# Latent attention rewritten with keys on the partitions: row maxima from a separate product, the shift as two contraction rows, no turning of the probabilities

## The chip, the cores and the metric

The kernel runs on one core of a Trainium2 chip. The metric is the device time of one execution in microseconds (us), the median of several runs. The engines are called PE (matrix product; PEld is its weight load), DVE (vector), ACT (activation), POOL (GpSimd) and SP (the queue that issues most DMAs). Each engine works through its instructions in the order in which the program was written out for it.

## The reference

The reference is a two-layer decoder trunk. Layer 0 mixes tokens with a windowed attention, layer 1 with a multi-head latent attention, and each mixer is followed by a mixture of experts. Only the latent attention is touched. It computes, for 16 heads over 2048 tokens, with queries and keys of 64 + 32 features and values of 64:

```
q = concat(q_nope, rope(q_rope)); k = concat(k_nope, rope(k_rope, shared by all heads))
sc = einsum('bqhd,bkhd->bhqk', q, k) * 96 ** -0.5
sc = where(kpos <= qpos, sc, -inf)
p = softmax(sc, axis=-1)
o = einsum('bhqk,bkhd->bqhd', p, v);  out = o.reshape(b, s, 1024) @ w_o
```

## The kernel before

All products are made from float16 pairs: a number is kept as a high part and a low part, and a product is three matmuls (high by high, high by low, low by high). The latent attention has two parts. `latents` makes the compressed latents, the queries (left in DRAM as `q`) and the shared rotary keys (`kr`). `attend`, which the change rewrites, loops over heads.

In `attend` a unit is one head `h` and one tile `i` of 128 queries; queries lie on the partitions. `scores` makes the scores of a unit in chunks of up to 512 keys: three matmuls into a PSUM bank (`sc`, a ring of 7 that `room` hands out), a fourth on the diagonal that adds the causal mask, and a maximum over the chunk on DVE (L1401). When the last chunk is there, a second small maximum joins them (L1406), and only then ACT takes the exponential with the negated maximum as its bias (L1410, `bpr`). The second product needs keys on the partitions, so the probabilities are turned. Four fifths of them are split first, high part by DVE or ACT (L1425, L1427), low part by POOL or DVE (L1428), packed (`bpp`) and turned by a DMA from SBUF to SBUF (`send`, L186, `bpt`). One fifth (`direct`) is turned by PE (`turn_unit`, L1440), and then split from PSUM by ACT and DVE (L1444, L1445, `bpd`). `values` runs LAG = 6 units behind: for each block of 128 keys one matmul of the high part with 130 columns and one of the low part with 65 (L1459, L1460) into `po`, which DVE sums over its two halves (L1466).

Keys and values of the next pair of heads are projected in between (`pair`, its matmuls are L202 to L204, its splits L177 and L182), in the rooms of the same ring. `finish` divides by the sums, turns and stores a pair of heads to `ob`; `deliver` loads a head's queries into `qb` from DRAM. The list `todo` spreads these pieces over the units.

The program text gives instructions their priority. A planner then writes out each engine's order beforehand, and may bring forward an instruction that it takes to be ready. On the chip every engine keeps that order.

Of the kernel before, what the change touches and what calls it, by code (L numbers as in the profile page):

```python
# [20 lines left out]
S, D = 2048, 1024  # L21
# [105 lines left out]
class Kernel:  # L127
# [994 lines left out]
    def mla(self, x1_d, y_d, x2_d, d, keep):  # L1122
# [17 lines left out]
        with self.tc.tile_pool(name="hw", bufs=2, side="right", reuse_waits="tile") as self.hw:  # L1140
            self.latents(x1_d, y_d, x2_d, d["kr"], d["q"])
            self.attend(d["q"], d["kr"], d["ob"], rooms)
# [186 lines left out]
    def attend(self, q_d, kr_d, o_d, w_o):  # L1329
        nc, tc = self.nc, self.tc  # L1330
        V, G, C = nc.vector, nc.gpsimd, nc.scalar
        LAG, PACK, SHARES, TURNED = 6, 8, (2 / 5, 1 / 16), 1 / 5
        with ExitStack() as s:
# [4 lines left out]
            kb = [self.t(kp, [96, 2, S], F16, f"kb{n}") for n in range(3)]  # L1338
            qb = [self.t(kp, [96, 2, S], F16, f"qb{n}") for n in range(2)]
            for n in range(3):  # L1340
                nc.sync.dma_start(kb[n][NOPE:], kr_d)
            U, heads, todo, owed = {}, {}, [], [0.0, -150.0, 0.0]

            pack = {"n": 0}

            def room():
                return self.t(ps, [P, 512], F32, "sc", bufs=7)

            def place(nb):
                if pack["n"] + nb > PACK:  # L1350
                    send()
                if pack["n"] == 0:
                    pack["pp"] = self.t(wk, [P, PACK, 2, P], F16, "bpp", bufs=8)
                    pack["pt"] = self.t(wk, [P, PACK, 2, P], F16, "bpt", bufs=9)
                at = pack["n"]
                pack["n"] += nb
                return pack["pp"][:, at:at + nb], pack["pt"][:, at:at + nb]

            def send():
                n, pp, pt = pack["n"], pack["pp"], pack["pt"]  # L1360
                if n:
                    self.turn(pt[:, :n].rearrange("p k s q -> p (k s) q"), pp[:, :n].rearrange("p k s q -> p (k s q)"))
                pack["n"] = 0
# [9 lines left out]
            def direct(h, i, w):  # L1373

                owed[2] += TURNED * w
                if h == B_H - 1 and i >= 13:
                    return True
                if owed[2] > w / 2:
                    owed[2] -= w
                    return True  # L1380
                return False

            def scores(n, h, i, u, c):

                (Qh, Ql), (Kh, Kl) = ([b[h % len(b)][:, x] for x in range(2)] for b in (qb, kb))
                qs = slice(i * P, (i + 1) * P)
                nk = (i + 1) * P
                ncn = -(-nk // 512)
                if c == 0:
                    u["sm"], u["sc"], u["pt"], u["pr"] = self.t(wk, [P, 8], F32, "bsm2", bufs=4), [], [], []  # L1390
                sm = u["sm"]
                w = min(512, nk - 512 * c)
                ks = slice(512 * c, 512 * c + w)
                sc = room()
                last = c == ncn - 1
                nc.tensor.matmul(sc[:, :w], Qh[:, qs], Kh[:, ks], start=True, stop=False)  # L1396
                nc.tensor.matmul(sc[:, :w], Qh[:, qs], Kl[:, ks], start=False, stop=False)  # L1397
                nc.tensor.matmul(sc[:, :w], Ql[:, qs], Kh[:, ks], start=False, stop=not last)  # L1398
                if last:
                    nc.tensor.matmul(sc[:, w - P:w], self.ident_b, self.causal, start=False, stop=True)  # L1400
                V.tensor_reduce(sm[:, c:c + 1], sc[:, :w], axis=AX.X, op=ALU.max, negate=ncn == 1)  # L1401
                u["sc"].append((sc, w))
                if not last:
                    return
                if ncn > 1:
                    V.tensor_reduce(sm[:, 4:5], sm[:, 0:ncn], axis=AX.X, op=ALU.max, negate=True)  # L1406
                nm = sm[:, 4:5] if ncn > 1 else sm[:, 0:1]
                for sc, w in u["sc"]:
                    pr = self.t(wk, [P, 512], F32, "bpr", bufs=7)
                    C.activation(pr[:, :w], sc[:, :w], AF.Exp, bias=nm)  # L1410
                    if direct(h, i, w):
                        u["pr"].append((len(u["pt"]), pr, w))
                        u["pt"].append(None)
                        continue
                    pp, pt = place(w // P)
                    u["pt"].append(pt)
                    pb = pr[:, :w].rearrange("p (k q) -> p k q", q=P)

                    mine = [False, False]
                    for part, share in enumerate(SHARES):  # L1420
                        owed[part] += share * w
                        if owed[part] > w / 2 and not (part and mine[0]):
                            mine[part], owed[part] = True, owed[part] - w
                    if mine[0]:
                        V.tensor_copy(pp[:, :, 0], pb)  # L1425
                    else:
                        C.activation(pp[:, :, 0], pb, AF.Copy)  # L1427
                    (V if mine[1] else G).tensor_tensor(pp[:, :, 1], pb, pp[:, :, 0], op=ALU.subtract)  # L1428
                if n % 2 and (h == B_H - 1 or n == len(units) - 1):
                    send()  # L1430

            def turn_unit(u):

                many = len(u["pr"]) > 1
                for c, pr, w in u["pr"]:
                    if many and c % 2 == 0:
                        two = self.t(wk, [P, PACK, 2, P], F16, "bpt", bufs=9)
                    tp = room()
                    for k in range(0, w, P):
                        nc.tensor.transpose(tp[:, k:k + P], pr[:, k:k + P], self.ident)  # L1440
                    out = two[:, c % 2 * 4:] if many else self.t(wk, [P, 4, 2, P], F16, "bpd", bufs=5)
                    out = u["pt"][c] = out[:, :w // P]
                    tp = tp[:, :w].rearrange("p (k q) -> p k q", q=P)
                    C.activation(out[:, :, 0], tp, AF.Copy)  # L1444
                    V.tensor_tensor(out[:, :, 1], tp, out[:, :, 0], op=ALU.subtract)  # L1445

            def values(h, i, n, u, c):

                second = n % 2
                j = units[n ^ 1][1]  # L1450
                if c == 0 and not second:
                    U["po"] = self.t(ps, [P, 512], F32, "po", bufs=1)
                slot = i > j
                po = U["po"][:, slot * 130:(slot + 1) * 130]
                v = self.vbs[h // 2 % 2]
                pt = u["pt"][c]
# [52 lines left out]
            for n in range(len(units) + LAG):  # L1509
# [24 lines left out]
                for c in range(max(ns, nv)):  # L1534
                    if c < ns:
                        scores(n, h, i, U[n], c)
# [121 lines left out]
```

## Time and profile before

| | |
|---|---|
| median of 3 runs | 3584.36 us (3579.23 to 3592.11) |
| the profiled execution | 3587.38 us, of which the span of the profile is 3585.3 us |
| mean granted PE clock | 0.928 of full speed |
| busy in the span | PE 2972.7, DVE 2785.0, ACT 2105.8, POOL 1564.5 us |
| latent attention (`attend`) | about 1684 to 2550 us of the span |

Busy time is the union of an engine's instructions. PE's matmuls overlap one another, so the distance between two starts, not the duration, is what a matmul costs in a stream. The DMA share is the mean busy share of the core's 16 DMA engines.

### The profile page before, as it was taken

What the parts mean: (1) busy time and instruction counts of PE and PEld (TensorE: products, weight loads), DVE (VectorE), ACT (ScalarE), POOL (GpSimd) and SP (SyncE); (2) the same over time, 40 slices, a digit from 0 to 9 for tenths busy, and PEclk for the clock granted to TensorE, in tenths of its full rate; (3) what the DMA queues carried; (4) which work ended last, traced back from release to release, by engine and by line L of the source; (5) the groups of instructions that cost most, each with busy time, mean ns of one, the idle gap of its engine ahead of it and who ended that gap; (6) DMA issues with size and microseconds to landing.
All of it is one profiled execution on the core that took longest, in us unless ns stands there. A gap on an engine that the chain in (4) does not pass through costs nothing. (4 is left out here: it accounts for less than half of the span.)

```text
span 3585.3 us, 82401 instructions
## 1 busy us (share of the span) xinstructions
PE 2972.7 (83%) x32611; PEld 2239.8 (62%) x32611; DVE 2785.0 (78%) x5288; ACT 2105.8 (59%) x3669; POOL 1564.5 (44%) x1562
## 2 busy tenths in 40 slices
PE   7888888599989885798888888897887699989960
PEld 3445444399988884344666656565443699988860
DVE  5777758797888787775787878788687788877858
ACT  6766621166667675554777777677311566677743
POOL 3544425323332235664576666666244123233245
PEclk9999989799999998898999999999998799999985
DMA  7887679799999998986899999999698899999996
GB/s 209 169 175 156 128 221 324 236 348 348 333 366 342 360 367 273 245 231 169 150 186 183 165 167 178 163 182 192 168 281 270 266 348 355 360 358 367 358 346 246
DMA packets 1107572, 922.13 MB, mean 257 GB/s; under 512 B 933120, under 2 KB 991744, under 8 KB 1056256
## 3 DMA queue, kind: packets, MB, share of 16 engines
q1 hardware_dynamic: 1073504, 808.67, 84.0%
q0 software_dynamic: 33664, 108.03, 8.3%
q8 instruction: 259, 4.24, 0.5%
q14 instruction: 145, 1.19, 0.1%
HBM read 538.33 MB, written 150.21 MB: 192 GB/s over the span
## 5 line engine op out<-in xcount | busy, mean ns | idle before, releaser
L182 DVE SCALAR_TENSOR_TENSOR wl<-raw,wh 128x2048 f16<-128x2048 f32 x322 | 844.7, 2628 | 161.2 <-ACT wh L177 158.1
L915 PE MATMUL pg<-xt,wh 128*128 128x128 f16 (+5 forms) x4096 | 818.5, 230 | 54.7 <-DMA xt<-xs 47.5
L917 PE MATMUL pg<-xt,wl 128*128 128x128 f16 (+5 forms) x4096 | 806.6, 230 | 44.3 <-DVE wl L182 44.1
L916 PE MATMUL pg<-xt,wh 128*128 128x128 f16 (+5 forms) x4096 | 817.8, 230 | 0.0
L177 ACT ACTIVATE wh<-raw 128x2048 f16<-128x2048 f32 x384 | 721.0, 1900 | 85.9 <-DMA raw<-in_moe_w_dram 76.8
L1428 POOL TENSOR_TENSOR bpp<-bpr,bpp 128x512 f16<-128x512 f32 (+3 forms) x448 | 474.3, 1076 | 276.2 <-DVE bpp L1425 169.7
L945 POOL DMA_DIRECT2D y<-yr x256 | 144.5, 571 | 707.2 <-DVE yr L937 556.3
L935 PE MATMUL py<-hh,wl 128*128 128x128 f16 (+5 forms) x2048 | 419.5, 232 | 36.1 <-POOL wl L180 36.0
L917 PEld LDWEIGHTS <-wl 128*128 128x128 f16 x4096 | 402.6, 99 | 55.1 <-DVE wl L182 54.8
L1401 DVE TENSOR_REDUCE bsm<-sc 128x1 f32<-128x512 f32 (+3 forms) x640 | 372.8, 600 | 78.4 <-PE sc L1398 63.1
L915 PEld LDWEIGHTS <-wh 128*128 128x128 f16 x4096 | 405.1, 99 | 40.1 <-issue 30.8
L934 PE MATMUL py<-hl,wh 128*128 128x128 f16 (+5 forms) x2048 | 418.6, 232 | 11.0 <-DVE hl L180 11.0
L933 PE MATMUL py<-hh,wh 128*128 128x128 f16 (+5 forms) x2048 | 417.8, 232 | 1.9 <-ACT wh L177 1.2
L916 PEld LDWEIGHTS <-wh 128*128 128x128 f16 x4096 | 405.1, 99 | 17.2 <-issue 17.2
L1410 ACT ACTIVATE bpr<-sc,bsm 128x512 f32<-128x512 f32 (+3 forms) x640 | 352.0, 630 | 98.2 <-DVE bsm L1406 93.5
L180 POOL TENSOR_TENSOR wl<-raw,wh 128x2048 f16<-128x2048 f32 x62 | 254.0, 4096 | 271.7 <-ACT wh L177 192.8
L1459 PE MATMUL po<-v,bpt 128*128 128x130 f16 x1750 | 208.3, 224 | 77.9 <-DMA bpt<-bpp 67.7
L1396 PE MATMUL sc<-kb,qb 96*128 96x512 f16 (+3 forms) x640 | 233.2, 364 | 28.3 <-ACT bpr L1410 12.8
L935 PEld LDWEIGHTS <-wl 128*128 128x128 f16 x2048 | 204.2, 100 | 53.7 <-POOL wl L180 41.5
L1397 PE MATMUL sc<-kb,qb 96*128 96x512 f16 (+3 forms) x640 | 231.4, 362 | 0.0
L1398 PE MATMUL sc<-kb,qb 96*128 96x512 f16 (+3 forms) x640 | 229.9, 361 | 0.0
L1459 PEld LDWEIGHTS <-bpt 128*128 128x128 f16 x1750 | 161.8, 99 | 107.4 <-DMA bpt<-bpp 90.5
(327 smaller groups left out, 7793.9 us busy)
## 6 DMA issues: line engine op xcount, KB each, us to landing
raw<-in_moe_w_dram SPq DMA_DIRECT2D x384, 1024.0 KB
y<-yr POOLq DMA_DIRECT2D x144, 160.0 KB, 9.0
x<-pxr SPq DMA_DIRECT2D x32, 512.0 KB
cz<-x SPq DMA_DIRECT2D x32, 512.0 KB
xs<-zero SPq DMA_DIRECT2D x32, 384.0 KB
q<-qn SPq DMA_DIRECT2D x48, 256.0 KB
y<-yr POOLq DMA_DIRECT2D x72, 128.0 KB, 7.8
ax<-in_x_t_dram SPq DMA_DIRECT2D x16, 512.0 KB
```

The lines of the kernel that those rows point to most:

```text
L177: nc.scalar.activation(hi, src, AF.Copy, scale=scale)
L182: eng.scalar_tensor_tensor(lo, src, scale, hi, op0=ALU.mult, op1=ALU.subtract)
L915: nc.tensor.matmul(out, hi, x[:, c], start=c == 0, stop=False)
L916: nc.tensor.matmul(out, hi, x[:, KC + c], start=False, stop=False)
L917: nc.tensor.matmul(out, lo, x[:, c], start=False, stop=c == KC - 1)
L933: nc.tensor.matmul(out, hi, hh[:, m], start=m == 0, stop=False)
L934: nc.tensor.matmul(out, hi, hl[:, m], start=False, stop=False)
L935: nc.tensor.matmul(out, lo, hh[:, m], start=False, stop=m == F // P - 1)
L1401: V.tensor_reduce(sm[:, c:c + 1], sc[:, :w], axis=AX.X, op=ALU.max, negate=ncn == 1)
L1410: C.activation(pr[:, :w], sc[:, :w], AF.Exp, bias=nm)
L1428: (V if mine[1] else G).tensor_tensor(pp[:, :, 1], pb, pp[:, :, 0], op=ALU.subtract)
L1459: nc.tensor.matmul(po, pt[:, k % 4, 0], vv, start=k == 0, stop=False)
```

## The change

Scores are now made with keys on the partitions: the stationary operand is a block of 128 keys, the moving operand up to 512 queries. A step is a head, a group `g` of 512 queries and a pair `j` of key blocks; there are 20 steps in a head and 320 in all. The three matmuls of a block go into one half of a two-bank PSUM tile `st` (2 buffers), ACT takes the exponential of both halves in one instruction where no diagonal is in the way, and the split result (`bpt`) is already in the form that the second product reads. The shares of DVE are 0.3 of the high parts and 0.08 of the low parts; ACT and POOL do the rest.

The maximum of a query is no longer on hand when the exponential is taken, so it comes from a product of its own: `maxima` makes high by high alone, with queries on the partitions, in 40 chunks a head, two chunks a step, AHEAD = 32 chunks in front. When half a head (8 query tiles) has its maxima, `shifts` negates them, splits them into two float16 numbers, turns them on PE, stores them in DRAM (`shift`) and loads them into two more rows of `qb`, 96 and 97; the matching rows of `kb` hold 256 and 1. The first matmul of a block thus contracts over 98 rows and subtracts the maximum by itself.

PSUM is now two banks for `sc` (maxima, projections, small turns), four for `st` and two for `po0` and `po1`. `kb` has 4 buffers instead of 3. The pieces that were in `todo` have fixed steps.

```diff
+        LAG, AHEAD, SHARES = 6, 32, (0.3, 0.08)
...
+            kb = [self.t(kp, [R + 2, 2, S], F16, f"kb{n}") for n in range(4)]
+            qb = [self.t(kp, [R + 2, 2, S], F16, f"qb{n}") for n in range(2)]
+            for k in kb:
+                nc.sync.dma_start(k[NOPE:R], kr_d)
+                G.memset(k[R:R + 2, 0], 1.0)
+                G.memset(k[R:R + 1, 0], 256.0)
...
-                return self.t(ps, [P, 512], F32, "sc", bufs=7)
+                return self.t(ps, [P, 512], F32, "sc", bufs=2)
...
+            def maxima(h, i, c):
+                Qh, Kh = qb[h % 2][:R, 0], kb[h % 4][:R, 0]
+                w = min(512, (i + 1) * P - 512 * c)
+                last = 512 * c + w == (i + 1) * P
+                if i % 8 == 0 and c == 0:
+                    M[h] = self.t(wk, [P, 8, 4], F32, "bmx", bufs=3)
+                    G.memset(M[h], NEG)
                 sc = room()
+                mm(sc[:, :w], Qh[:, i * P:(i + 1) * P], Kh[:, 512 * c:512 * c + w], start=True, stop=not last)
                 if last:
+                    mm(sc[:, w - P:w], self.ident_b, self.causal, start=False, stop=True)
+                V.tensor_reduce(M[h][:, i % 8, c:c + 1], sc[:, :w], axis=AX.X, op=ALU.max)
+                if last and i % 8 == 7:
+                    shifts(h, i // 8)
+
+            def shifts(h, half):
+                nm = self.t(wk, [P, 8], F32, "bnm")
+                V.tensor_reduce(nm, M[h], axis=AX.X, op=ALU.max, negate=True)
...
+                V.tensor_scalar(hi, nm, 1.0 / 256, None, op0=ALU.mult)
+                V.tensor_copy(ab[:, 0], hi)
+                V.scalar_tensor_tensor(ab[:, 1], ab[:, 0], -256.0, nm, op0=ALU.mult, op1=ALU.add)
+                tp, row = room()[:16, :P], self.t(wk, [16, P], F16, "brow")
+                nc.tensor.transpose(tp, ab.rearrange("p s t -> p (s t)"), self.ident)
+                V.tensor_copy(row, tp)
...
+                    nc.sync.dma_start(shift_d[h, u, cs].rearrange("(t k) -> t k", k=P), row[8 * u:8 * u + 8])
+                nc.sync.dma_start(qb[h % 2][R:R + 2, 0, cs], shift_d[h, :, cs])
+
+            def scores(u, h, g, j):
+                (Qh, Ql), (Kh, Kl) = ([b[:, x] for x in range(2)] for b in (qb[h % 2], kb[h % 4]))
+                st = self.t(ps, [P, 2, 512], F32, "st", bufs=2)
+                pr = self.t(wk, [P, 2, 512], F32, "bpr", bufs=4)
+                pt = u["pt"] = self.t(wk, [P, 2, 2, 512], F16, "bpt", bufs=LAG + 3)
...
+                for e in range(2):
+                    b = 2 * j + e
+                    at = max(0, b - 4 * g) * P
...
+                    mm(out, Kh[:, ks], Qh[:, qs], start=True, stop=False)
+                    mm(out, Kh[:R, ks], Ql[:R, qs], start=False, stop=False)
+                    mm(out, Kl[:R, ks], Qh[:R, qs], start=False, stop=not diagonal)
+                    if diagonal:
+                        mm(st[:, e, at:at + P], self.causal, self.ident_b, start=False, stop=True)
+                        parts.append((slice(e, e + 1), at))
+                for es, at in parts or [(slice(0, 2), 0)]:
+                    src, hi, lo = pr[:, es, at:], pt[:, 0, es, at:], pt[:, 1, es, at:]
+                    C.activation(src, st[:, es, at:], AF.Exp)
...
                     if mine[0]:
+                        V.tensor_copy(hi, src)
                     else:
+                        C.activation(hi, src, AF.Copy)
+                    (V if mine[1] else G).tensor_tensor(lo, src, hi, op=ALU.subtract)
...
-            def turn_unit(u):
...
+            def values(u, h, g, j):
+                if j == 0:
+                    po[h, g] = [self.t(ps, [P, 512], F32, f"po{n}") for n in range(2)]
...
+                        mm(out, pt[:, 0, e, qs], vv, start=b == 0 and n % 2 == 0, stop=False)
+                        mm(out[:, :HD + 1], pt[:, 1, e, qs], vv[:, :HD + 1], start=False, stop=n % 2 == 1 and b == 4 * g + n)
...
+            for n in range(len(steps) + LAG):
+                h, at = divmod(n, each)
+                if at == 0 and h + 1 < B_H:
+                    deliver(h + 1)
...
+                while done < min(len(chunks), 2 * n + AHEAD):
+                    maxima(*chunks[done])
+                    done += 1
+                if n < len(steps):
                     U[n] = {}
+                    scores(U[n], *steps[n])
                 if n >= LAG:
+                    values(U.pop(n - LAG), *steps[n - LAG])
+                if n in todo:
+                    todo.pop(n)()
```

## Rows read from the trace of the kernel before

**Rows 1.** Windows: length, busy by engine, granted clock, DMA share, GB/s.
```profile
1684.00:1700.00 16.00, 9.84 (x34) 4.64 (x35) 8.85 (x16) 7.23 (x12) 4.68 (x4) 0.64 0.42 136
...
2100.00:2200.00 100.00, 89.62 (x999) 61.93 (x998) 86.56 (x194) 77.62 (x154) 70.08 (x72) 1.00 1.06 182
...
2400.00:2500.00 100.00, 77.17 (x753) 49.94 (x751) 80.22 (x174) 70.60 (x137) 62.69 (x61) 0.91 0.96 187
...
sum 866.00, PE 747.64 PEld 508.26 DVE 706.02 ACT 625.65 POOL 544.09; mean PE 74.76 PEld 50.83 DVE 70.60 ACT 62.57 POOL 54.41
```

**Rows 2.** DMA in the stage: packets, MB, share; issues with count.
```profile
q1 hardware_dynamic: 491117, 144.53, 95.7%
...
bpt<-bpp SPq DMA_TRANSPOSE x240
```

**Rows 3.** Waits in the stage: who waited for whom, us, times, longest.
```profile
POOL bpp L1428 <- DVE bpp L1425: 169.7, 110, 10.1
ACT bpr L1410 <- DVE bsm L1406: 93.5, 87, 4.0
...
PE po L1459 <- DMA bpt<-bpp: 67.7, 48, 4.1
...
PE sc L1396 <- ACT bpr L1410: 12.8, 19, 1.7
...
PE sc L1396 <- DVE bpd L1445: 7.1, 8, 2.4
```

**Rows 4.** Instructions in order of time on PE: start, us, operation, shapes.
```profile
1908.58 0.63 PE L1440 MATMUL sc<-ident,bpr 128*128 128x128 f32 x4
...
1909.05 0.27 PE L1396 MATMUL sc<-kb,qb 96*128 96x256 f16 x1
...
1909.43 0.38 PE L1396 MATMUL sc<-kb,qb 96*128 96x512 f16 x1
...
1910.08 0.22 PE L1459 MATMUL po<-v,bpd 128*128 128x130 f16 x1
...
1910.17 0.22 PE L1459 MATMUL po<-v,bpd 128*128 128x130 f16 x1
...
1910.61 0.22 PE L1459 MATMUL po<-v,bpt 128*128 128x130 f16 x1
```

**Rows 5.** Groups by line on PE in the stage: busy, mean ns, idle before.
```profile
L1440 PE MATMUL sc<-ident,bpr 128*128 128x128 f32 x448 | 78.7, 287 | 2.1 <-DVE bsm L1406 1.1 <-ACT bpr L1410 0.5 <-DVE bpt L1445 0.5
```

**Rows 6.** Groups by line on DVE in the stage.
```profile
L1401 DVE TENSOR_REDUCE bsm<-sc 128x1 f32<-128x512 f32 (+3 forms) x640 | 372.8, 600 | 78.4 <-PE sc L1398 63.1 <-PE sc L1400 9.2 <-PE po L1460 4.3
L1425 DVE CAST bpp<-bpr 128x512 f16<-128x512 f32 (+3 forms) x201 | 118.2, 589 | 23.0 <-ACT bpr L1410 21.3 <-issue 1.2
L1445 DVE TENSOR_TENSOR bpd<-sc,bpd 128x512 f16<-128x512 f32 (+3 forms) x144 | 77.8, 540 | 5.8 <-ACT bpd L1444 5.0
...
L1428 DVE TENSOR_TENSOR bpp<-bpr,bpp 128x512 f16<-128x512 f32 (+3 forms) x36 | 29.6, 823 | 0.3 <-ACT bpp L1427 0.2
L1406 DVE TENSOR_REDUCE bsm<-bsm 128x1 f32<-128x3 f32 (+2 forms) x192 | 27.7, 144 | 1.2
```

**Rows 7.** Groups by line and shape in the stage: POOL's subtraction.
```profile
L1428 POOL TENSOR_TENSOR bpp<-bpr,bpp 128x512 f16<-128x512 f32 x345 | 401.4, 1176 | 242.5 <-DVE bpp L1425 143.4 <-ACT bpp L1427 42.6 <-DVE bsm L1406 15.5
...
L1428 POOL TENSOR_TENSOR bpp<-bpr,bpp 128x128 f16<-128x128 f32 x26 | 12.5, 481 | 8.4 <-DVE bpp L1425 7.2 <-POOL bpp L1428 0.8 <-PE sc L1440 0.2
```

**Rows 8.** Instructions in order of time, DVE and POOL side by side.
```profile
2506.32 0.41 DVE L1425 CAST bpp<-bpr 128x512 f16<-128x512 f32 x1
...
2506.81 1.15 POOL L1428 TENSOR_TENSOR bpp<-bpr,bpp 128x512 f16<-128x512 f32 x1 [1.06 <-DVE bsm L1406]
...
2507.12 0.93 DVE L1425 CAST bpp<-bpr 128x128 f16<-128x128 f32 x1
```

**Rows 9.** DMA issues of the whole span: the median from issue to landing.
```profile
cy<-y,iy POOLq DMA_INDIRECT x64, 6.4
```

More of the change, by code (lines that the diff above doesn't have):

```diff
@@ L1141, in mla @@
             self.latents(x1_d, y_d, x2_d, d["kr"], d["q"])
-            self.attend(d["q"], d["kr"], d["ob"], rooms)
+            self.attend(d["q"], d["kr"], d["shift"], d["ob"], rooms)
         return rooms
@@ L1336, in attend @@
             ps = s.enter_context(tc.tile_pool(name="tp", bufs=1, space=PSUM, reuse_waits="tile"))
[L1338 to L1344, printed above, removed]
-            def room():
-                return self.t(ps, [P, 512], F32, "sc", bufs=7)
[L1349 to L1363, printed above, removed]
+            kb = [self.t(kp, [R + 2, 2, S], F16, f"kb{n}") for n in range(4)]
[4 more added lines that the diff above has]
+                G.memset(k[R:R + 1, 0], 256.0)
+            U, M, heads, po, todo, owed = {}, {}, {}, {}, {}, [0.0, -150.0]
+            def room():
+                return self.t(ps, [P, 512], F32, "sc", bufs=2)
             def deliver(h):
@@ L1401, in scores @@
[L1401 to L1417, printed above, removed]
+                    mm(sc[:, w - P:w], self.ident_b, self.causal, start=False, stop=True)
@@ L1424, in scores @@
                     if mine[0]:
-                        V.tensor_copy(pp[:, :, 0], pb)
+                        V.tensor_copy(hi, src)
                     else:
[L1427 to L1430, printed above, removed]
-            def turn_unit(u):
[L1434 to L1456, printed above, removed]
-                for k in range(4 * c, min(4 * c + 4, i + 1)):
-                    vv = v[:, k, h % 2]
-                    nc.tensor.matmul(po, pt[:, k % 4, 0], vv, start=k == 0, stop=False)
-                    nc.tensor.matmul(po[:, :HD + 1], pt[:, k % 4, 1], vv[:, :HD + 1], start=False, stop=k == i)
-                if second and 4 * c + 4 > i:
-                    if n % NT == 1:
-                        heads[h] = self.t(wk, [P, NT, HD + 1], F32, "ou", bufs=3)
-                    lo, hi = min(i, j), max(i, j)
-                    V.tensor_reduce(heads[h][:, lo:hi + 1:hi - lo], U["po"][:, :260].rearrange("p (u s f) -> p u f s", u=2, s=2),
-                                    axis=AX.X, op=ALU.add)
-                    if h == B_H - 1:
-                        if n % 4 == 3:
-                            todo.insert(0, lambda q=n % NT // 4: finish(h // 2, q))
-                    elif h % 2 and n % NT == NT - 1:
-                        todo[0:0] = [lambda q=q: finish(h // 2, q) for q in range(4)]
@@ L1501, in project_weights @@
                     self.split(w_o[0][c][:, n:n + 512], w_o[1][c][:, n:n + 512], raw, WS)
-            order = [x for n in range(NT // 2) for x in (NT - 1 - n, n)]
-            units = [(h, i) for h in range(B_H) for i in (order if h < B_H - 1 else range(NT))]
+            steps = [(h, g, j) for h in range(B_H) for g in range(4) for j in range(2 * g + 2)]
+            chunks = [(h, i, c) for h in range(B_H) for i in range(NT) for c in range(i // 4 + 1)]
+            each, done = len(steps) // B_H, 0
             deliver(0)
@@ L1549 @@
+            assert not todo
 INS = ["x", "a_w_in", "a_sinks", "a_w_o", "b_w_down", "b_q_norm", "b_kv_norm", "b_w_uq", "b_w_ukv", "b_w_o",
@@ L1561, in scratch @@
     d["kr"] = k.t(pool, [ROPE, 2, S], F16, "kr")
+    d["shift"] = k.t(pool, [B_H, 2, S], F16, "shift")
     return d
```

105 lines of the change are left out of this document (43 added, 62 removed).

## The prediction

> **What bounds the kernel now.** The table of slices shows where the latent attention lies; the views below are of that stretch alone, because the change touches nothing else. I first read the windows [rows 1]: 866 us from 1684 to 2550, in which PE is busy 747.6, DVE 706.0, ACT 625.7 and POOL 544.1 us. No compute engine is full, and the reader should see that PE lies idle for 118 us. The DMA view comes next [rows 2]: the hardware queue took 95.7% of 16 engines, in the main for 240 turning transfers of `bpp` into `bpt`. The waits agree [rows 3]: PE's longest is for just that transfer, 67.7 us in 48 waits, and the others are small beside it. So the stage goes at the pace of the turning, and PE is second.
>
> What PE needs is not its busy time. From starts in a full-speed stream [rows 4]: three score matmuls of 512 columns take 1910.08 - 1909.43 = 0.65, so 0.217 us each; five pairs of value matmuls take 0.44, so 0.088 a pair; four PE transposes take 1909.05 - 1908.58 = 0.47, so 0.12 each. The code gives the counts. A head has 17,408 causal columns per product (136 blocks of 128 by 128), so 16 heads and three products have 835,584, or 354 us. 2176 value pairs are 191 us, 256 masks of 128 columns (0.054 each) 14 us, 448 transposes [rows 5] 54 us, and the projections of seven pairs of heads, 168 matmuls of 512 and 672 of 128 columns, 73 us. The sum is 686 us. The stage thus has 866 - 686 = 180 us that are not PE work at full speed: 118 of idleness and 62 in which matmuls ran at the lower clock or drained before a gap. In the window 2400 to 2500 the granted clock averages 0.91, in 2100 to 2200 it is 1.00 [rows 1].
>
> **The change part by part.** *The turning goes.* The DMA wait of 67.7 us [rows 3] goes with it, since what `values` reads is now written by engines alone. The 448 PE transposes go: 54 us. So does PE's wait for a room held by a turned chunk, 7 us [rows 3].
>
> *Scores with keys on the partitions.* The same causal columns, 40 blocks a head in place of 40 chunks, three matmuls and as many weight loads each: no difference on PE. Two more contraction rows add no columns; no row shows 98 rows beside 96, and I take nothing (a block's cost would follow its columns, as in [rows 4]).
>
> *The separate maxima.* One more product over all causal columns is a third of 354, so 118 us; 256 more masks are 14 us; 32 small transposes at 0.12 are 4 us. PE's need becomes 686 - 54 + 118 + 14 + 4 = 768 us, 82 more than before. That is the price of the change, and it is about what the lost wait and the lower clock cost now. DVE's maxima stay 640 in number and 373 us in sum [rows 6].
>
> *DVE.* The busy time 706 us loses the turned subtractions (78), the small maxima (28), and the old casts and subtractions (118 and 30) [rows 6], which leaves 452. The new casts have 0.3 of 278,528 columns, 83,600. Alone, 512 columns take 0.41 us [rows 8], so they need 67 us. But a cast of 128 columns that began inside a POOL subtraction lasted 0.93 us and ended when that did (2506.81 + 1.15 = 2507.96) [rows 8]. It had to wait. POOL's pieces get twice as long, so each of about 134 casts may wait between nothing and 2.3 us (twice 1.15): 0 to 308 us. Today's 201 casts have 87,400 columns, so they would need 70 us alone and took 118, or 0.24 us of waiting each; doubled this is 0.48, and I take 67 us. The low parts have 0.08 of the columns, 22,300, against 13,400 now at 30 us: 50 us. The 32 turns of the shift cost some six small instructions of 0.144 us [rows 6], 28 us. DVE comes to 452 + 67 + 67 + 50 + 28 = 664 us, below PE.
>
> The Trainium skill (GPSIMD Engine Reference, section Specifications) says that POOL's SBUF interfaces are shared with the vector engine and collide with its two-port modes and with its instructions of two SBUF inputs. The trace agrees for the cast: 0.93 us against 0.41 for four times the columns [rows 8]. If every cast paid in full, DVE would have 905 us by this rule instead of 664; that is a rival below.
>
> *POOL and ACT.* POOL subtracts 0.92 of the columns where it did 0.74. From [rows 7], 384 more columns cost 0.695 us, so 1024 columns cost 1.176 + 0.927 = 2.1. 177 such pieces are 372 us, 236 of the diagonal pieces at 0.83 (the middle of the two rows) 196, and `finish` 70: about 640 us. ACT takes the same columns in fewer, larger instructions, and its share of the copies stays at 0.7, so it has no more than its 626 us [rows 1]. Its 93.5 us of waiting for a unit's maximum [rows 3] were slack and end, since the maximum now comes in by PE.
>
> *The shift's way.* `shifts` is two legs through DRAM. No row has so small a transfer; the nearest is a gather of 6.4 us from issue to landing [rows 9], so the way costs at most 13 us, and nothing if hidden. The first half of a head's maxima is complete ten steps before it is needed. The second half is emitted with step 4 of its head and needed at step 6, about 3 us of PE work later. What waits behind it on PE is that step's scores and through them ACT and POOL; what the planner can put there are the values of up to six steps (4 us) and later maxima. So the wait is 0 to 10 us a head, 0 to 160 us in all. I take 0.6 a head, 10 us, nearer to the hidden end, because the ready work covers the nearest part.
>
> *The start.* The first 16 us now have 9.8 us of PE work [rows 1]. Twelve maxima of up to 0.68 us on DVE and one way of the shift go ahead of the first scores, partly beside them; I take 6 us, with 0 to 15 as the bounds. *Buffers.* The room ring falls from 7 banks to 2, so PE stands still when DVE is two maxima behind. PE's present wait for ACT to free a room, 12.8 us [rows 3], is the nearest row; I leave it as it is, with 0 to 60 as the bounds. The wider `oT` and `op` and the memsets lie on queues with slack; I take nothing for them, as their cover is POOL's and SP's idle time.
>
> **The sum.** PE's need 768; of the 118 us of idleness 118 - 68 - 7 = 43 stay, and 10 and 6 come: 59; of the 62 us of lower clock and drains I keep a third, 20, since the waits for the DMA made over half of the gaps. That gives 847 us against 866, a gain of 19. The profiled execution took 3587.4 us, 3.0 above the median of the runs, so the forecast is 3587.4 - 19 - 3 = 3565 us.
>
> **The rivals.** *Nothing much is left idle (faster still).* PE has work at hand at nearly all times and keeps 1.00 of its clock; a span of 768 + 16 + 16 = 800 us, the gain 66, the time about 3518. For it: the shares of DVE, ACT and POOL in 800 us stay at or below 83%. Against it: the start and the tail of the stage don't shrink.
>
> *PE stops in short gaps and its clock falls (slower).* With two rooms and two score tiles, each late maximum or exponential stops PE. If the granted clock is 0.91 over the whole stage, as in 2400 to 2500 [rows 1], PE's need becomes 768 / 0.91 = 844, and with 59 of idleness 903 us: 37 more, the time about 3621. It decides from a granted clock under 0.95 (768 / 0.95 + 59 = 867). Against it: 2100 to 2200 has PE busy 89.6% with gaps in it, and 1.00 [rows 1]. The Trainium skill (TensorE: Matmul & The Clock Gate, section A second HAM failure mode) names this very pattern, cycling through PSUM with small idle gaps, as a reason for a clock that swings.
>
> *DVE becomes the bound.* With the full 308 us of waiting DVE has 905 us, and the stage 905 + 16 = 921: 55 more, the time about 3639. At half of it DVE has 751, still below PE. It decides from 200 us of waiting on, 1.5 us a cast. For it: [rows 8]. Against it: today's mean wait is 0.24.
>
> **How the numbers follow.** Within 0.3% (11 us) is about what a measurement of this kernel can't tell from no change: 3574 to 3595. My forecast has 0.44: with its bounds it runs from 3545 to 3600, 0.28 of it faster and 0.16 the same. The faster rival has 0.26, all faster. The clock has 0.18: 0.03 the same, 0.15 slower. DVE has 0.12, all slower. That makes faster 0.54, the same 0.19, slower 0.27. The range leaves out a tenth on each side: 3518, the gain of the faster rival, to 3622, just past the clock's price.
>
> **What would show it.** No `bpt<-bpp` transfer, and a DMA share far under one half in the stage. PE with 82 us more work and, as the most loaded engine, over 90% busy; granted clock at 0.97 or more. Casts of some 1.0 us on DVE at 1024 columns, with their maxima well above, and POOL pieces of 2.1 us. PE's longest wait is for DVE's maxima, or for the shift's load at step 6 of each head. The forecast is wrong if that wait is over 3 us a head, if the clock falls below 0.95, or if DVE is busy for over 90% of the stage.

## The result: 3818.24 us, 6.4% slower

The changed kernel takes 3818.24 us (median of 4 runs, 3803.04 to 3820.64), the kernel before in the same runs 3588.24 us: a ratio of 1.0636, 95% interval 1.0602 to 1.0671. The forecast was 3565 us in a range of 3518 to 3622; the measured time lies outside it, and the change loses 230 us.

**The stage.** The latent attention, from 1684 us on, ends at about 2547 us in the trace of before and at 2783 us in that of after (the end of its last value product). So all of the loss is in it. First the windows of the changed kernel (length, busy by engine with instructions, granted clock, DMA share, GB/s); [rows 1] answers to them.

```profile
1684.00:2783.00 1099.00, 912.60 (x8296) 547.22 (x8296) 773.21 (x1306) 576.56 (x932) 647.62 (x506) 0.87 0.16 37
...
2100.00:2200.00 100.00, 87.85 (x907) 56.19 (x905) 77.08 (x127) 58.91 (x100) 68.18 (x54) 0.94 0.15 31
...
2600.00:2700.00 100.00, 79.80 (x600) 44.29 (x599) 68.90 (x116) 46.79 (x73) 51.80 (x38) 0.79 0.25 67
```

No engine is full, as before. PE's busy time rose from 747.6 to 912.6 us, its idleness from 118 to 186 (1099 - 913), and the granted clock over the stage is 0.87. In 2600 to 2700 PE ran 600 matmuls where a window at 1.00 has about 1000 [rows 1]. The turning of the probabilities is gone: the hardware DMA queue has 15.5% of the engines where it had 95.7% [rows 2].

```profile
q1 hardware_dynamic: 57902, 41.04, 15.5%
```

The waits of the changed kernel in the stage (who waited for whom, us, times, longest), beside [rows 3]:

```profile
ACT bpr L1414 <- PE st L1408: 184.1, 88, 16.0
POOL bpt L1425 <- ACT bpt L1424: 166.3, 38, 16.9
...
POOL bmx L1369 <- DVE bnm L1381: 117.9, 15, 13.5
...
PE sc L1371 <- DVE bmx L1374: 75.1, 116, 5.0
...
PE sc L1387 <- DVE bab L1385: 54.5, 32, 4.0
...
PE sc L1371 <- DVE qn L182: 14.3, 1, 14.3
...
PE st L1406 <- DMA qb<-shift: 11.0, 10, 5.1
```

The wait for `bpt<-bpp` has gone. In its place PE waits 116 times for DVE's maxima, that is, for a room, and 32 times for the shift's last small instruction. Most telling are ACT and POOL: ACT waits up to 16.0 us at a stretch for one block of scores, and POOL behind ACT up to 16.9. These waits are not spread out.

**One such stretch.** Windows of 5 us on the changed kernel, and PE's instructions in order of time (start, us, shapes, idle before and who ended it):

```profile
2590.00:2595.00 5.00, 4.95 (x79) 4.55 (x77) 3.47 (x9) 2.40 (x5) 0.67 (x2) 0.82 0.16 56
...
2600.00:2605.00 5.00, 2.86 (x8) 0.76 (x7) 3.73 (x7) 1.26 (x2) 0.61 (x1) 0.50 0.79 211
2605.00:2610.00 5.00, 2.86 (x9) 0.79 (x8) 4.23 (x10) 0.63 (x1) 0.12 (x1) 0.50 0.15 52
2610.00:2615.00 5.00, 4.38 (x16) 1.78 (x15) 2.97 (x7) 0.00 (x0) 0.00 (x0) 0.50 0.01 2
2615.00:2620.00 5.00, 5.00 (x16) 1.92 (x15) 0.89 (x2) 3.10 (x3) 1.69 (x1) 0.59 0.00 0
2620.00:2625.00 5.00, 5.00 (x51) 3.17 (x50) 2.14 (x4) 4.30 (x5) 4.37 (x3) 1.00 0.00 0
```

```profile
2602.72 1.01 PE L1371 MATMUL sc<-kb,qb 96*128 96x512 f16 x2 [1.66 <-DVE bmx L1374]
2604.09 1.07 PE L1371 MATMUL sc<-kb,qb 96*128 96x512 f16 x2 [0.35 <-DVE bmx L1374]
...
2606.82 1.18 PE L1371 MATMUL sc<-kb,qb 96*128 96x512 f16 x2 [0.32 <-DVE bmx L1374]
...
2609.73 0.38 PE L1387 MATMUL sc<-ident,bab 128*16 128x128 f32 x1 [1.62 <-DVE bab L1385]
...
2613.37 0.58 PE L1406 MATMUL st<-qb,kb 98*128 98x512 f16 x1
```

PE makes maxima alone, two at a time, since there are two rooms, and then waits for DVE (75% and 85% busy). ACT stops; the clock is at its lower level (0.50, that is 1.2 GHz), so that even the products run at half speed. Only when the transpose of the shift is through (2609.73) may the next scores start (2613.37). With scores running again the clock is at 0.59 in the window from 2615 and at 1.00 in that from 2620.

There is one such burst in every head. Group `g` = 2 (step 6) needs the second half's maxima. From the second score block of step 5 to the first of step 6, PE ran 288 of the 640 maxima, and these 16 stretches last 350.7 us in sum; PE is idle for 116 us of this time. Counted in the trace at head 8, the maxima run 11 chunks behind the place where the program text has them at step 0 and 13 behind at step 5; at step 6 it is 3. Other heads are further behind: from 10 to 21 chunks at step 5 of heads 1 to 14. This number of chunks is called the debt below, and the burst is the debt being paid. The debt is a count in PE's own order, and on the chip every engine keeps the order that the planner wrote out; so the planner, with two rooms to give, wrote the maxima late, and what the chip adds are the waits. The large pieces are near the size foreseen: 192 POOL pieces of 1024 columns at 2.14 us, casts on DVE at 1.22 us (all widths), maxima at 373 us in [rows 6] and 372 now.

```profile
L1425 POOL TENSOR_TENSOR bpt<-bpr,bpt 128x1024 f16<-128x1024 f32 x192 | 409.9, 2144 | 253.9 <-ACT bpt L1424 166.3 <-DVE bpt L1422 49.7 <-issue 26.9
```

```profile
L1374 DVE TENSOR_REDUCE bmx<-sc 128x1 f32<-128x512 f32 (+3 forms) x640 | 372.2, 603 | 197.0 <-PE sc L1371 122.6 <-PE sc L1373 58.9 <-PE po L1439 9.1
L1422 DVE CAST bpt<-bpr 128x1024 f16<-128x1024 f32 (+4 forms) x118 | 143.8, 1219 | 33.9 <-ACT bpr L1414 33.1 <-issue 0.2
...
L1384 DVE CAST bab<-bhi 128x8 f32<-128x8 f16 x32 | 28.0, 875 | 1.1
```

### The profile page after: what moved, and what is told of

It reads as the page before. It is cut to its first block, busy times and chain, and to the rows that moved or that the text cites. A ratio compares the mean times of both kernels' runs of the same rounds, so it can differ in the third digit from the quotient of the medians.

```text
span 3816.3 us, 82087 instructions
## 1 busy us (share of the span) xinstructions
PE 3139.2 (82%) x33068; PEld 2276.5 (60%) x33068; DVE 2845.8 (75%) x5045; ACT 2057.4 (54%) x3368; POOL 1684.5 (44%) x1538
## 5 line engine op out<-in xcount | busy, mean ns | idle before, releaser
L182 DVE SCALAR_TENSOR_TENSOR wl<-raw,wh 128x2048 f16<-128x2048 f32 x322 | 840.6, 2615 | 150.8 <-ACT wh L177 150.0
L1425 POOL TENSOR_TENSOR bpt<-bpr,bpt 128x1024 f16<-128x1024 f32 (+4 forms) x384 | 570.1, 1503 | 282.7 <-ACT bpt L1424 166.3
L1374 DVE TENSOR_REDUCE bmx<-sc 128x1 f32<-128x512 f32 (+3 forms) x640 | 372.2, 603 | 197.0 <-PE sc L1371 122.6
L1414 ACT ACTIVATE bpr<-st 128x1024 f32<-128x1024 f32 (+2 forms) x448 | 292.7, 686 | 277.4 <-PE st L1408 184.1
L915 PEld LDWEIGHTS <-wh 128*128 128x128 f16 x4096 | 405.5, 99 | 40.1 <-issue 30.8
L1371 PE MATMUL sc<-kb,qb 96*128 96x512 f16 (+3 forms) x640 | 242.7, 398 | 99.1 <-DVE bmx L1374 75.1
L1438 PE MATMUL po<-v,bpt 128*128 128x130 f16 x2176 | 256.8, 223 | 7.5 <-DVE ou L1446 7.5
L1406 PE MATMUL st<-qb,kb 98*128 98x512 f16 (+3 forms) x640 | 238.4, 373 | 12.8 <-DMA qb<-shift 11.0
L1439 PE MATMUL po<-v,bpt 128*128 128x65 f16 x2176 | 237.6, 195 | 6.8 <-POOL bpt L1425 4.8
L1407 PE MATMUL st<-qb,kb 96*128 96x512 f16 (+3 forms) x640 | 237.9, 372 | 0.0
```

Source lines behind the costliest of these rows:

```text
L182: eng.scalar_tensor_tensor(lo, src, scale, hi, op0=ALU.mult, op1=ALU.subtract)
L915: nc.tensor.matmul(out, hi, x[:, c], start=c == 0, stop=False)
L1374: V.tensor_reduce(M[h][:, i % 8, c:c + 1], sc[:, :w], axis=AX.X, op=ALU.max)
L1414: C.activation(src, st[:, es, at:], AF.Exp)
L1425: (V if mine[1] else G).tensor_tensor(lo, src, hi, op=ALU.subtract)
L1438: mm(out, pt[:, 0, e, qs], vv, start=b == 0 and n % 2 == 0, stop=False)
```

## Experiments on the cause

The theories were: A, two rooms are too few, so the maxima fall behind; B, the way of the shift through DRAM is too long; C, POOL holds up DVE; D, POOL's fills of `bmx` hold up the maxima. "Burst sum" below is the sum of the 16 stretches from step 5 to step 6, read from each trace as above. Ratios stand where a kernel was timed in rounds; the other times are of one execution. The edits are shown by their main lines.

**e3: a third room.** The scores give up a bank: three one-bank tiles, each with an exponential of its own.

```diff
-                return self.t(ps, [P, 512], F32, "sc", bufs=2)
+                return self.t(ps, [P, 512], F32, "sc", bufs=3)
...
-                st = self.t(ps, [P, 2, 512], F32, "st", bufs=2)
+                st = [self.t(ps, [P, 512], F32, "st", bufs=3) for _ in range(2)]
...
-                for es, at in parts or [(slice(0, 2), 0)]:
+                for es, at in parts:
```

> Three rooms in place of two, paid for by score tiles of one bank (three of them, each with its own exponential). Theory A (with two rooms the maxima fall behind the scores, so that between steps 5 and 6 of each head, in a stretch of some 22 us, PE runs a row of maxima and no scores): the maxima keep up, what is left between these steps is the way of the shift, and the time falls by 120 to 200 us to 3620 to 3700. Theory B (the way of the shift through DRAM is what is waited for): it stays, within 30 us of 3818. Theory C (VectorE is held up by POOL's subtractions): no gain, within 30 us, as the shares of the engines are the same.

Measured: 3634.65 us, 1.0138 (1.0097 to 1.0179) of the kernel before; 183 us of the 230 are back. The burst sum falls to 164.8 us, the debt at head 8's step 5 to 2 chunks, and PE's wait for maxima from 75.1 to 20.2 us, as the waits of e3 show:

```profile
PE sc L1371 <- DVE bmx L1374: 20.2, 37, 4.6
PE sc L1387 <- DVE bab L1385: 18.7, 15, 4.6
PE po L1438 <- DVE ou L1446: 14.6, 21, 1.7
```

**e7: the scores' half of e3 alone.** One-bank score tiles, four of them, and two rooms.

```diff
-                st = self.t(ps, [P, 2, 512], F32, "st", bufs=2)
+                st = [self.t(ps, [P, 512], F32, "st", bufs=4) for _ in range(2)]
```

> The changed kernel, two rooms as it is, but each score block of 512 has a one-bank tile of its own (four of them, the same four banks) and an exponential of its own: the half of e3 that is not the third room. Theory A (the gain of e3 is the third room for maxima): 3780 to 3840 us, and VectorE's maxima are still what TensorE waits for most, 60 us or more. Rival E (the gain of e3 came from the scores' own banks, freed one at a time): 3620 to 3720 us. Both half: 3720 to 3780 us.

Measured: 3790.14 us, burst sum 366.7 us. The split gives 28 us, so the room itself is worth about 155 (3790 - 3635), even with one bank less for the scores. PE's wait for the maxima stays at 72.4 us.

**e2: the maxima earlier.**

```diff
-        LAG, AHEAD, SHARES = 6, 32, (0.3, 0.08)
+        LAG, AHEAD, SHARES = 6, 40, (0.3, 0.08)
```

> AHEAD 40 in place of 32, so that the program text has the maxima four steps further in front. Theory A: where the text has them is not what holds them, the two rooms are; less than 30 us of change, 3790 to 3830, and the stretch between steps 5 and 6 stays at about 20 us. Theory B (two steps of lead are too few for the shift): six steps hide its way, a gain of 100 us or more, under 3720.

Measured: 3806.08 us, burst sum 354.4 us. The lead did not come through: at the start of step 6 of head 8 PE has made 362 maxima in e2 and 361 in after, and in all 16 heads of both no score stands between the transpose of the shift and step 6. So e2 agrees with A, that the place in the program text is not what holds the maxima, but it gave the shift no more time and does not test B. What speaks against B as the main cause is e3: there too no score stands between the two, and 183 us come back.

**e4: no maxima.** The maxima, the shift and its transfers are left out, and the exponent is scaled by 1/64.

```diff
-                while done < min(len(chunks), 2 * n + AHEAD):
-                    maxima(*chunks[done])
-                    done += 1
```

> Leaves out the maxima and the shift altogether (rows 96 and 97 of qb are 0); the exponent is scaled by 1/64 so that it stays finite, so the output is not the softmax. It prices what the maxima cost in all. Theory A and B: scores, exponentials and values alone run near PE's need of 686 - 54 + 0 = 632 us with little idleness, so a stage of 660 to 720 us against 866 before and a time of 3380 to 3445. Theory C: the casts and subtractions are the same, so the stage stays above 800 us and the time above 3520.

Measured: 3442.94 us. The maxima as built cost 375 us, against 132 us of PE work in the forecast. DVE's casts beside POOL are still there and the stage ends at 2417 us, after 733 (660 to 720 were expected, and over 800 by C); but DVE has little more than half its work there (426 us), so the better test of C is e6.

**e5: no fills.** Four fixed tiles for the maxima, filled once.

```diff
-                    M[h] = self.t(wk, [P, 8, 4], F32, "bmx", bufs=3)
-                    G.memset(M[h], NEG)
+                    M[h] = MM[i // 8 + 2 * (h % 2)]
```

> The tiles for the maxima are four fixed ones, filled once at the start, so POOL has no fill in the loop and doesn't wait there for VectorE. Theory D (POOL's 118 us of waiting at these fills hold up the subtractions and through them the values): a gain of 60 to 118 us, 3700 to 3758. Theory A: POOL waits because the stretch between steps 5 and 6 has nothing for it; less than 20 us of change, 3798 to 3830.

Measured: 3818.43 us, the changed kernel's time. D is refuted, although POOL waits 117.9 us to fill in the trace of after: those waits cost nothing.

**e6: DVE relieved, two rooms.** All casts to ACT, all subtractions to POOL.

```diff
-        LAG, AHEAD, SHARES = 6, 32, (0.3, 0.08)
+        LAG, AHEAD, SHARES = 6, 32, (0.0, 0.0)
```

> The changed kernel with its two rooms, but VectorE casts and subtracts nothing (shares 0 and 0 in place of 0.3 and 0.08): ScalarE casts all, GpSimd subtracts all. About 144 and 50 us of VectorE's work go, and with them casts that wait for GpSimd. Theory A (two rooms let only two maxima be under way, and each takes its turn on VectorE): a maximum is held up less by other VectorE work, so some of the 230 us comes back, 3700 to 3790 us, but not the gain of the third room. Theory C (VectorE, held up by GpSimd, is what makes the maxima late): 3600 to 3680 us. If neither counts: 3810 or more.

Measured: 3763.04 us. 55 us return, as A had it, and the burst sum is 313.7 us. C, which asked for 3600 to 3680, is refuted as the main cause; and a maximum itself is not held up by POOL, as it takes 603 ns on average in after and 600 before [rows 6].

**c4: one ring of six for both.**

```diff
-                return self.t(ps, [P, 512], F32, "sc", bufs=2)
+                return self.t(ps, [P, 512], F32, "sc", bufs=6)
...
-                st = self.t(ps, [P, 2, 512], F32, "st", bufs=2)
+                st = [room() for _ in range(2)]
```

> Scores and maxima (and the projections) draw on one ring of six one-bank rooms in place of two for maxima and two times two for scores. Theory A (rooms alone set the loss): at or below three rooms' 3635 us, 3610 to 3645. Rival G (one ring hands rooms out in the order of the instructions, so a maximum waits behind a score block that ScalarE holds and the other way round): 3650 to 3750 us.

Measured: 3665.37 us, 1.0197 (1.0162 to 1.0232): in the range of rival G, and 31 us over e3 with the same banks. The wait that G names is hardly there, though: PE waits 2.1 us for ACT before its maxima and 0.9 for DVE's maxima before its scores. The burst sum is only 38.4 us, but PE now waits 20.3 us for DVE to empty the outputs, 19.0 for POOL and 30.8 for the shift's `bab` (e3: 14.6, 5.1 and 18.7). Sharing removes the bursts and adds other waits.

## Experiments on what was left

**c3: e3 with a lead of 40 chunks** (AHEAD = 40).

> Three rooms as in e3 (3635 us), and the maxima 40 chunks ahead of the scores in place of 32. Theory A (with three rooms the maxima keep their place, and what is left is TensorE's work): 3620 to 3645 us. Theory B (the shift's way through memory still holds the first block of a half): 3590 to 3620 us.

Measured: 3619.02 us, 1.0088 (1.0056 to 1.012): both ranges end at this value, and the run does not tell them apart.

**c1: c3 with a shift for every 512 queries** in place of 1024, without the fill.

```diff
-                if last and i % 8 == 7:
-                    shifts(h, i // 8)
+                if last and i % 4 == 3:
+                    shifts(h, i // 4)
```

> Three rooms, 40 chunks ahead, and the shift made for 512 queries at a time in place of 1024, so 64 small chains in place of 32, and no fill by GpSimd. Theory A: what is left over the kernel before is the maxima's own work on TensorE, so 3610 to 3640 us, within 15 us of the same without quarters. Theory F (the wait for a half's maxima still makes the bursts): 3580 to 3610 us.

Measured: 3711.31 us, 1.0325 (1.0282 to 1.0368): worse than either theory had it, 92 us over c3. The waits of c1 tell part of it: PE stands behind twice as many small chains on DVE. The maxima also run 20 to 28 chunks behind in head 8, where they run 5 to 15 behind in c3.

```profile
PE sc L1386 <- DVE bab L1384: 61.2, 46, 3.7
PE st L1405 <- DMA qb<-shift: 34.6, 20, 4.8
```

**d1 and d2: c3 with less for DVE.** d1 has SHARES = (0.15, 0.0), d2 (0.0, 0.0).

> Three rooms, 40 chunks ahead (3619 us), and VectorE casts 0.15 of the columns in place of 0.3 and subtracts none in place of 0.08. Theory A (TensorE's own work is the bound now, and what is left idle comes from stretches in which VectorE is full): 3590 to 3615 us. Theory H (VectorE's load does not matter any more): 3612 to 3630 us. Rival (ScalarE or GpSimd becomes late): 3630 or more.

> As d1, with VectorE casting nothing: ScalarE has all copies, about 60 us more than in d1. Theory A: 3585 to 3615 us, level with d1 or a little under. Rival (ScalarE becomes late, since it makes the exponentials and all copies, over 85% busy): 3620 to 3660 us.

Measured: d1 3594.73 us, 1.0032 (1.0014 to 1.0051); d2 3630.13 us, 1.0127 (1.008 to 1.0173). So DVE's load still counted (24 us from c3 to d1). In d2, whose time is in the range of the rival on ACT, ACT has all copies, but is not full (75 to 84% in the windows from 1800 to 2600). PE's wait for the shift's `bab` rises to 41.4 us, and the small scaling on L1383 takes 1396 ns on average, where it took 371 in after.

**d3: d1 with the shift's three small copies on ACT**, and the low parts of the output weights on POOL.

```diff
-                V.tensor_scalar(hi, nm, 1.0 / 256, None, op0=ALU.mult)
-                V.tensor_copy(ab[:, 0], hi)
+                C.activation(hi, nm, AF.Copy, scale=1.0 / 256)
+                C.activation(ab[:, 0], hi, AF.Copy)
...
-                V.tensor_copy(row, tp)
+                C.activation(row, tp, AF.Copy)
```

> As d1, with the three small copies of the shift on ScalarE (they took VectorE 0.3 to 0.7 us each beside GpSimd), and the low parts of the output weights on GpSimd in place of VectorE. Theory A with B's rest (TensorE stands 25 to 45 us behind the transposes of the shift): 3570 to 3595 us. Rival (ScalarE's queue is longer than VectorE's, so the shift comes later): 3610 to 3650 us.

Measured: 3601.99 us, 1.0049 (1.0024 to 1.0074): no gain over d1; neither range holds it.

**e8: d1 without the maxima**, cut as in e4.

> d1 (three rooms, lead 40, shares 0.15 and 0; 3595 us) without the maxima and the shift: their products, masks, VectorE's maxima and the transfers are left out, the exponent is scaled by 1/64. Theory A (with rooms enough the maxima cost about what the prediction's sum gave them: 118 + 14 + 4 us of TensorE's work and some 16 of start and waits): 140 to 165 us less, 3430 to 3455. Rival (they still cost far more than their work, by waits): below 3410 us.

Measured: 3476.19 us, 118 less than d1, below the 140 expected. But e8 is no clean floor: as in d1, POOL makes all subtractions, and now it is full, as the windows of e8 show; e4, where DVE has a share of them, is 33 us faster. A floor without POOL's limit would lie lower, so 118 us is a lower bound of what the maxima cost in d1.

```profile
1900.00:2000.00 100.00, 95.79 (x1052) 63.13 (x1051) 31.81 (x56) 86.49 (x189) 100.00 (x106) 1.00 0.19 43
```

**f3: d1 with the way through DRAM made twice.**

> d1 with the shift's way through memory made twice, one after the other (three more transfers for each half head). Theory A (the way is hidden behind a lead of a whole head, but for the first one): 3595 to 3612 us. Theory B (the way is on the path of every head): each of 32 ways costs some 4 to 6 us more, so 3640 or more.

Measured: 3619.99 us, 1.0087 (1.0068 to 1.0105), so about 20 us by the ratios, 0.6 us for each of the 32 ways: between the theories. PE's wait for the shift's load rises from 5.6 to 8.5 us only, for its transposes from 12.7 to 27.3. Through what the transfers hold up the transposes stays open.

**f2 and f1: the fill on DVE, and then the transposes a step later.** f2 is d1 with the first edit, f1 has both.

```diff
-                    G.memset(M[h], NEG)
+                    V.memset(M[h], NEG)
...
-                tp, row = room()[:16, :P], self.t(wk, [16, P], F16, "brow")
+                late.append(lambda: send(h, half, ab))
+
+            def send(h, half, ab):
+                tp, row = room()[:16, :P], self.t(wk, [16, P], F16, "brow")
...
+                due = len(late)
                 while done < min(len(chunks), 2 * n + AHEAD):
                     maxima(*chunks[done])
                     done += 1
+                for _ in range(due or (n == 0) * 2):
+                    late.pop(0)()
```

> d1 with the fill of the maxima's tile on VectorE in place of GpSimd, where the first fill stands behind the last rotated queries. Theory A: only the start gains, the 3.4 us that VectorE waits there for the fill and the 4.6 us that TensorE waits behind it, so 3586 to 3593 us. If the fills do not matter: 3592 to 3598.

> As f2, and each shift's transpose and transfers are written one step behind its maxima, so that VectorE's small chain is done when TensorE comes to the transpose (it waits there 12.7 us in d1, 4.6 of them at the start, where nothing changes). Theory A: up to 8 us under f2, 3578 to 3590. Rival (the order on TensorE puts the transpose where VectorE is ready anyway, and the shift comes later): 3588 to 3605.

Measured: f2 3587.68 us, 1.0007 (0.9995 to 1.002); f1 3570.05 us, 0.9958 (0.9936 to 0.9981). f2 is where it was expected; f1 is faster than either of its ranges and beats the kernel before by 0.4%. Its burst sum is 11.1 us (f2: 95.3), so the later transposes also undid the bursts that were left. The expectation had put its gain on DVE's small chain; in the order written out there is more: f1 has at least one step of scores, mostly two or three, between the transpose of a half and the step 6 that needs it, where f2 has none in 8 of 16 heads. The windows and the waits of f1:

```profile
1684.00:2550.00 866.00, 804.90 (x8305) 524.71 (x8304) 639.57 (x1258) 665.55 (x1336) 709.82 (x730) 0.96 0.21 47
...
2100.00:2200.00 100.00, 97.80 (x1045) 65.17 (x1045) 75.59 (x151) 82.77 (x165) 88.23 (x92) 1.00 0.18 39
```

```profile
PE sc L1372 <- DVE qn L182: 13.8, 1, 13.8
PE sc L1372 <- DMA qb<-q: 13.5, 10, 3.2
PE sc L1372 <- DVE bmx L1375: 8.3, 5, 6.2
```

**g1: f1 with two rooms again; g2: f1 with four.** g1 puts back the changed kernel's `sc` and `st`; g2 has `sc` with 4 and `st` with 2 buffers.

> f1 with the changed kernel's two rooms and two two-bank score tiles put back; lead 40, shares 0.15 and 0, fill on VectorE and late transposes stay. Theory A (without a third room the other edits help little): 3710 to 3770 us, bursts of maxima between steps 5 and 6 again, 250 us or more in sum. Rival (lead, shares and late transposes were the cure): 3570 to 3640 us.

> f1 with four rooms and two one-bank score tiles in place of three and three. Theory A (three rooms were enough, and the scores with two single banks now wait for ScalarE): 3590 to 3680 us. Rival (rooms are still short): 3550 to 3568 us.

Measured: g1 3737.53 us, burst sum 280.1 us and a debt of 18 chunks at head 8's step 5; the other edits without the third room and the split give only 81 us, with them 248. g2 3644.36 us, 1.0176 (1.0136 to 1.0217): 74 us over f1. There PE waits 4.9 us for DVE's maxima and 10.1 for ACT to free a score tile, but 40.8 us, in 14 waits, for the load of queries:

```profile
PE sc L1372 <- DMA qb<-q: 40.8, 14, 4.2
PE sc L1372 <- DVE qn L182: 14.4, 1, 14.4
PE st L1410 <- ACT bpr L1418: 10.1, 20, 1.2
```

That four rooms lose is shown. That the scores' two tiles are the way they lose is not: the longest wait is another one.

## Why the prediction was wrong

**The step that failed is *Buffers*.** It took the row of today's wait for a room, 12.8 us [rows 3], for a ring that falls from 7 banks to 2, and gave 0 to 60 us as bounds. That row was read from a ring with five more banks, where ACT gave the room back, and says nothing of one with two. In its place the runs showed about 155 us for the third room by itself and 183 together with the scores' split (e7, e3); taking both from f1 costs 167 (3737.53 - 3570.05). In the terms of the sum, PE's need of 768 us was to be joined by 59 of idleness and 20 of lower clock and drains. In after the idleness is 186 us, 116 of it in the bursts, and PE's busy time is 145 over the need (913 - 768). The prediction did see that "PE stands still when DVE is two maxima behind", but priced the stops, not what they lead to: with two rooms a chunk can be made only when DVE has finished the one before last, and DVE's queue holds a 1.2 us cast or 0.7 us splits ahead of it. That account of the stops is argued from the durations; the debt of 10 to 21 chunks that came with them is counted. It is due at step 6 of each head, where ACT has nothing else to do. The range did not carry the prediction's own bounds either: 60 us for the rooms in place of 12.8, 160 for the shift's way in place of 10 and 15 for the start in place of 6 would have added 206 us to the forecast.

**The lower clock: rival right in direction, not in place or size.** The rival on short gaps had 0.91 over the stage and 3621 us. The granted clock is 0.87 in after and 0.96 in f1. It is lowest in and just behind the bursts: 0.76 over their 350.7 us (0.50 from 2600 to 2615) and 0.78 over the 10 us that follow each, against 0.95 in the rest of the stage. So most of it is lost there, and little in gaps all along. PE's busy time in the stage is 912.6 us in after and 804.9 in f1 for nearly the same number of matmuls, so 108 us of the loss are the same work at a lower clock or drained before a stop. The Trainium skill (TensorE: Matmul & The Clock Gate, section A second HAM failure mode) describes a clock that goes to and fro when PE stops briefly between groups of matmuls while it cycles through PSUM. The rows above agree, with 0.50 where PE stops after every two maxima and 1.00 where scores fill it.

**The maxima's work on PE: the term was nearly right.** 118 and 14 us were expected. In f1 the maxima's products take 129 us from one start to the next and their masks 19, without the gaps behind them, at a granted clock of 0.96. With all its edits the stage of f1 ends at 2547.2 us, 863 us after 1684; the sum said 847. Its idleness is 59 us, as the sum had it, and its busy time 36 over the need, where 20 were said. That the idleness fits is partly luck, since the terms in it are others: *the start* was taken at 6 us with 15 as the bound, and PE is idle from 1684 to 1740 us for 10 us in before, 30 in after and 25 in f1, so it cost 15 to 20. In after the first maxima wait 14.3 us for the last queries, and then for DVE's small chain; the first scores come at 1717.8 us, where they came at 1688.6 before. One count was a little short: the 448 transposes are those from 1690 to 2540 us, and the stage from 1684 to 2550 has 471, 3 us more.

**DVE and POOL.** *DVE* was put at 664 us; it is 773.2. The casts took 144 us against 134 (67 and 67), at 1.39 us for 1024 columns where 1.0 was said; low parts took 67 against 50. The small chain was priced at 0.144 us an instruction, 28 us. Its five instructions took 184, 371, 875, 618 and 278 ns on average, 74 us for 32 turns. The other 36 us come from the 452: whole durations were taken off 706 us of busy time, but DVE's instructions overlap, and in before their durations add up to 801. As for the small chain, a cast of 8 columns can be held up by POOL like any other. Here is one of the longest in after:

```profile
2630.44 2.12 POOL L1425 TENSOR_TENSOR bpt<-bpr,bpt 128x1024 f16<-128x1024 f32 x1
2630.55 2.04 DVE L1384 CAST bab<-bhi 128x8 f32<-128x8 f16 x1
...
2632.85 0.38 PE L1387 MATMUL sc<-ident,bab 128*16 128x128 f32 x1 [2.77 <-DVE bab L1385]
```

It ends 0.03 us after POOL's piece; the one in the burst, where POOL was idle, took 0.17 us (at 2609.30). PE waited 2.77 us behind it. The Trainium skill (GPSIMD Engine Reference, section Specifications) has POOL share its SBUF interfaces with the vector engine. The row agrees, and shows that instructions with hardly any data can be held up too. The rival in which DVE becomes the bound did not come about: it is 70% busy, though its load counted (e6 55 us, d1 24 us). *POOL and ACT* hold: 647.6 and 576.6 us, where 640 and at most 626 were said.

**The shift's way** was taken at 10 us with 0 to 160 as bounds: PE's wait for its load is 11.0 us. That step holds as a wait; but no score stands between the transpose and step 6 in any head, so in these 3.6 us or more PE had only the last maxima of the debt to make. What the prediction missed beside it is the wait for the transpose, 54.5 us in 32 waits: the chain of small instructions on DVE, which PE meets in order.

Two of the signs that were named for a wrong forecast are there: PE's wait for maxima is over 3 us a head (75.1 / 16 = 4.7), and the clock under 0.95.

**What stays open.** A ring's size changes the order written out as well as the waits on the chip, and no run has the one without the other: whether two rooms would do with an order that kept the maxima in place is not shown. Why c1 lost so much more than its waits show, through what f3's transfers delay the transposes, and why the four rooms of g2 wait for queries were not settled.

## What to carry to other kernels

When a change takes buffers from a ring, a wait read at the old size is no bound for the new one: work out how long one buffer is held, with everything that may stand ahead in its consumer's queue, and ask when the work that falls behind is due all at once. Look for the debt itself, in counts of items done at a fixed point of the loop, and not only for the engine's waits; here 75 us of waits stood for 183 us. Check in the trace that a lead written in the program text came through, before a run with it is read as a test. A product that runs ahead is only hidden if it has buffers enough to be mixed with the main stream; here three banks for it and three for the scores were best, two and four or four and two were slower.

## What was not expected of the hardware

A VectorE cast of 128 by 8 elements took 0.17 us alone and 2.04 us beside one GpSimd subtraction of 1024 columns; its 32 instances average 0.875 us. While TensorE was fed through two rooms alone, its granted clock went from 0.82 (2590 to 2595 us) to 0.50, and it was at 1.00 in the window from 2620 us, where scores filled it.
